# Samples' old states loaded four batches at a time, new states from spread rows on four row groups, behind the output projection

## The chip, the cores and the metric

The kernel runs on one core of a Trainium2 chip. The metric is the device time of one execution in microseconds (us), taken as the median of several runs. A core has five engines that each run their own list of instructions in order and wait for one another by semaphores: TensorE (PE in the profile, its weight loads PEld), VectorE (DVE), ScalarE (ACT), GpSimd (POOL) and SyncE (SP). In this kernel SP issues nearly all DMA transfers; a transfer that has to wait holds up all that stand behind it on SP.

## What is computed

One inference step of a decoder with two layers, width 1024. 256 new tokens of one prompt and 8 new tokens of each of 8 samples share all weights, so the kernel works on 320 tokens: columns 0 to 255 are the prompt, 256 to 319 the samples, 8 for each. Each layer projects its input, runs three mixers side by side (an SSD recurrence, a causal pooling, a sparse attention over a paged cache), projects their outputs back, and runs a convolutional FFN. The change lies in the SSD mixer, in what it does with the samples. Cut to that, for one sample `b`, with `x` of 8 heads by 64, `B` and `C` of 2 groups by 128, four heads to a group:

```
xc = x * dt                                       # 8 tokens
ac = dt * a
a_cum = cumsum(ac)
y_off = C . h0[b] * exp(a_cum)                    # old state, (8 heads, 64, 128)
y_diag = ((C . B^T) * exp(segsum(ac))) . xc
h_new[b] = h0[b] * exp(a_cum[-1]) + sum over the 8 tokens of B[t] * exp(a_cum[-1] - a_cum[t]) * xc[t]
y = (y_off + y_diag + d_skip * x) * silu(z), then rmsnorm
```

`h0[b]` comes in as `state_ssm`, `h_new[b]` goes out as `ssm_sample`. All is float32.

## The kernel before

A layer runs through these stages: norm and input projections; the mixers, interleaved by a list of steps (`ORDER`); `out_proj`, the output projection (eight tiles of 128 output rows, each 24 products `mt`: four inputs of pooling and attention first, the four of SSD behind); `ffn`. Weights come in tiles `raw` (four buffers) and are split on ACT and DVE into a high and a low part, `wh` and `wl`, or `wa` for the pair in one tile. While layer 0's `ffn` starts, `feed` also runs the cache compression of layer 1: PE products `cs` of `cache` tiles with the tiles `w` (loads on L461 and L830), which fill PE while the FFN's input is normalised.

The code goes through a scheduler: an engine's order comes from priorities that follow the program text, and `later(n)` puts what is written in its block behind work that is written up to n further on. `manual_schedule` keeps the order as written on the engine named. What stands in front on SP is thus settled when the kernel is built.

`ssd` goes through three chunks: two of the prompt, and one with the 64 sample tokens. In the third, the samples are taken in two halves `q` of four batches `j`. For each batch the old state `h` (128 rows of N by 512 columns, 256 KB) is loaded, and two products `yoh` (one for each group `g`) multiply it with the spread C rows `csp` into 32 rows of PSUM. After four batches ACT copies `yo`, PE transposes it (`yot`), and DVE scales it (`yof`) and adds it to the outputs. `ssd_norm` follows.

The new state takes `state_pre`: `bm`, the rows of B with a mask (columns `C_BM` of the constants) that leaves only one batch's 8 of 32 rows, and `hd`, the decay of the old state in place; and `state_add`: two products `sn` over 32 rows (32 of them the half's tokens, 24 of these zeros), an add `h<-h,sn` on DVE (for the keys `ha...` set to P a copy `sne` on ACT and an add on POOL), and the store `o_sss`. The helper lines in the rows: L283 matmul, L287 transpose, L290 tensor_tensor, L195 and L196 copies, L202 scaling.

The two layers differ. Layer 0 loads one batch at a time into `d2`, a pool of four buffers that other tiles share, and does everything for a batch in its turn in the third chunk. Layer 1 loads four batches with one transfer of 1 MB into `w8` (six buffers, shared with `cache`, `w`, `Ps`, `wa` and others), prepares `bm` and `hd` right there for both halves, does the first `j` of new states (`NE = 1`) in front of `ssd_norm`, and the other three behind `out_proj`, inside the start of the FFN.

A PSUM tile for these steps comes from `sst`, which takes pools in turn: `big` and `sd` in layer 0, `ns` and `sd` in layer 1.

Of the kernel before, what the change touches and what calls it, by code (L numbers as in the profile page):

```python
# [8 lines left out]
for _n, _w in (("ID", 128), ("ONE", 128), ("P", 1), ("TRI", 128), ("TRIU", 128), ("TRIS", 64), ("TRIUS", 64), ("GM", 128), ("SEL", 256),   # L9
               ("CAU", 128), ("CMP", 32), ("HS", 12), ("NEW", 8), ("WOLD", 8), ("COS", 24), ("SIN", 24), ("RW", 2),  # L10
               ("IC", 32), ("FOLD", 15), ("J1", 14), ("BM", 4), ("B8", 8)):
# [14 lines left out]
def constants():  # L26
# [38 lines left out]
    c[:96, C_BM:C_BM + 4] = (p[:96] % 32)[:, None] // 8 == np.arange(4)[None]  # L65
# [107 lines left out]
def build(ctx, tc, nc, A):  # L173
# [471 lines left out]
    def ssd(c):  # L645
# [15 lines left out]
        for i, (t0, n, tri, triu) in enumerate(CH):  # L661
# [67 lines left out]
            else:  # L729
# [5 lines left out]
                for q in range(2):  # L735
                    ph = sst(c, "yoh")
                    if l:
                        hq = w8_p.tile([128, 4, 512], F32, name="h0", tag="w8")
                        SP.dma_start(hq, A["s_ssm"][l][:, 4 * q:4 * q + 4])
                    for j in range(4):  # L740
                        if l:
                            h = hq[:, j]
                        else:
                            h = d2("h0")
                            SP.dma_start(h, A["s_ssm"][l][:, 4 * q + j])
                        c.h0[4 * q + j] = h
                        for g in range(2):
                            mm(ph[32 * j:32 * j + 32, 256 * g:256 * g + 256],
                               csp[:, g, 8 * (4 * q + j):8 * (4 * q + j) + 32], h[:, 256 * g:256 * g + 256])
                        if l == 0:  # L750
                            state_add(c, state_pre(c, bn, El, j, (q,)), xde, j, (q,))
# [12 lines left out]
                if l:  # L764
                    c.xde = xde
                    with later(SPR):
                        c.bm = [state_pre(c, bn, El, j, (0, 1)) for j in range(4)]

    def state_pre(c, bn, El, j, qs):

        bm = d1("bm")
        r = slice(32 * qs[0], 32 * qs[-1] + 32)
        sc(f"bm{c.l}{j}{qs[0]}", "D", bm[r], bn[r], cst[r, C_BM + j:C_BM + j + 1])
        for q in qs:
            h = c.h0[4 * q + j]
            tt(en(f"hd{c.l}{j}{q}", "P"), hp(h), hp(h), El[:, 1 + 4 * q + j, :, None].to_broadcast([128, 8, 64]), OP.mult)
        return bm

    def state_add(c, bm, xde, j, qs):

        pn = {q: sst(c, "sn") for q in qs}
        for g in range(2):
            for q in qs:
                r = slice(32 * q, 32 * q + 32)
# [12 lines left out]
    def states(c, js):  # L797
        for j in js:
            state_add(c, c.bm[j], c.xde, j, (0, 1))
# [531 lines left out]
```

## Time and profile before

| | |
|---|---|
| median of three runs | 1232.06 us (1231.94 to 1237.4) |
| profiled execution | 1224.47 us, of which 1222.3 us are the span |
| granted TensorE clock, mean | 0.97 |
| PE busy | 1171.7 us, 96% |
| DVE busy | 802.5 us, 66% |
| ACT busy | 536.7 us, 44% |
| POOL busy | 302.5 us, 25% |
| moved by DMA | 180.18 MB |

The profile is of one execution. PEclk is the TensorE clock that was granted, as a share of full speed (2.4 GHz; the lower level is 1.2 GHz). A float32 product shows as two records in the timeline, so "x4" of `yoh` or `sn` is two products. In a row of the timeline the matmuls are pipelined: the time of a group is from its first start to its last end.

### The profile page before, as it was taken

What the parts mean: (1) busy time and instruction counts of PE and PEld (TensorE: products, weight loads), DVE (VectorE), ACT (ScalarE), POOL (GpSimd) and SP (SyncE); (2) the same over time, 40 slices, a digit from 0 to 9 for tenths busy, and PEclk for the clock granted to TensorE, in tenths of its full rate; (3) what the DMA queues carried; (4) which work ended last, traced back from release to release, by engine and by line L of the source; (5) the groups of instructions that cost most, each with busy time, mean ns of one, the idle gap of its engine ahead of it and who ended that gap; (6) DMA issues with size and microseconds to landing.
All of it is one profiled execution on the core that took longest, in us unless ns stands there. A gap on an engine that the chain in (4) does not pass through costs nothing.

```text
span 1222.3 us, 23199 instructions
## 1 busy us (share of the span) xinstructions
PE 1171.7 (96%) x8450; PEld 1093.2 (89%) x8450; DVE 802.5 (66%) x1661; ACT 536.7 (44%) x950; POOL 302.5 (25%) x616
## 2 busy tenths in 40 slices
PE   7999998899999999999999999889999999999995
PEld 6799765599999999999999877778899999999995
DVE  4583667368756666656663688986685666666665
ACT  5445523236454444433433565433455444444431
POOL 4732222100513113311300033440342311111111
PEclk9999999699999999999999999898899999999998
DMA  7634227355555455545433445206345544445421
GB/s 277 191 100 137 76 85 252 100 161 185 175 177 199 167 168 181 159 146 184 156 104 105 154 131 189 99 27 199 119 138 171 165 143 159 152 145 158 150 72 43
DMA packets 85186, 180.18 MB, mean 147 GB/s; under 512 B 10449, under 2 KB 45009, under 8 KB 84049
## 3 DMA queue, kind: packets, MB, share of 16 engines
q1 hardware_dynamic: 84048, 176.61, 45.0%
q0 software_dynamic: 1024, 2.10, 0.6%
q8 instruction: 66, 1.08, 0.4%
q14 instruction: 48, 0.39, 0.1%
HBM read 168.97 MB, written 13.83 MB: 150 GB/s over the span
## 4 chain that ended last, share of the span: by engine, by line
PE 88%; DVE 5%; POOL 2%; ACT 2%; issue 1%; DMA 1%; SPq 1%; DVEq 0%; POOLq 0%; ACTq 0%
PE mt L283 67%; PE cs L283 5%; PE nat L283 4%; PE sn L283 1%; PE O L283 1%; PE sb L283 1%; PE sc L283 1%; PE yoh L283 1%; PE ss L283 1%; PE pe L283 1%; PE rb L283 1%; PE pT L287 1%; DMA h<-s_ssm 1%; PE sA L283 1%; DVE xt L437 1%
## 5 line engine op out<-in xcount | busy, mean ns | idle before, releaser
L342 ACT ACTIVATE wh<-raw 128x1024 fp32r<-128x1024 f32 (+2 forms) x156 | 159.9, 1026 | 199.7 <-PE mt L283 147.2
L283 PE MATMUL mt<-xh,wa 128*128 128x320 f32 x1024 | 237.2, 310 | 0.0
L283 PE MATMUL mt<-xl,wh 128*128 128x320 f32 x736 | 232.0, 315 | 0.0
L283 PE MATMUL mt<-xh,wl 128*128 128x320 f32 x736 | 231.2, 314 | 0.0
L283 PE MATMUL mt<-xh,wh 128*128 128x320 f32 x736 | 230.9, 315 | 0.2 <-ACT xh L421 0.2
L290 DVE TENSOR_TENSOR wl<-raw,wh 128x1024 fp32r<-128x1024 f32 (+2 forms) x151 | 179.5, 1189 | 68.2 <-ACT wh L342 65.5
L283 PEld LDWEIGHTS mt<-xh,wa 128*128 128x128 f32 x1024 | 174.8, 188 | 0.3
L283 PE MATMUL mt<-xl,wa 128*128 128x320 f32 x512 | 158.5, 310 | 0.0
L283 PEld LDWEIGHTS mt<-xh,wh 128*128 128x128 f32 x736 | 138.9, 189 | 5.8 <-issue 5.0
L283 PEld LDWEIGHTS mt<-xh,wl 128*128 128x128 f32 x736 | 138.8, 189 | 4.6 <-issue 3.9
L283 PEld LDWEIGHTS mt<-xl,wh 128*128 128x128 f32 x736 | 139.0, 189 | 3.2 <-issue 2.4
L290 DVE TENSOR_TENSOR wa<-raw,wa 128x1024 fp32r<-128x1024 f32 x92 | 113.5, 1234 | 37.2 <-ACT wa L342 36.9
L290 POOL TENSOR_TENSOR fa<-fa,fc 128x256 f32<-128x256 f32 (+1 forms) x128 | 82.0, 662 | 191.5 <-ACT fc L1171 136.8
L342 ACT ACTIVATE wa<-raw 128x1024 fp32r<-128x1024 f32 x92 | 96.8, 1053 | 48.4 <-DMA raw<-wg 34.9
L283 PE MATMUL mt<-act,wa 128*128 128x320 f32 x768 | 117.8, 309 | 0.0
L283 PEld LDWEIGHTS mt<-act,wa 128*128 128x128 f32 x768 | 114.0, 188 | 0.0
L283 PE MATMUL mt<-act,wh 128*128 128x320 f32 x512 | 113.2, 309 | 0.0
L283 PEld LDWEIGHTS mt<-xl,wa 128*128 128x128 f32 x512 | 96.3, 188 | 0.0
L1164 POOL COPY off<-fext 128x2 f32<-128x2 f32 x64 | 19.5, 304 | 283.2 <-DVE fext L290 283.2
L283 PEld LDWEIGHTS mt<-act,wh 128*128 128x128 f32 x512 | 85.6, 188 | 0.0
L290 DVE TENSOR_TENSOR fo<-fo,mt 128x320 f32<-128x320 f32 x112 | 54.0, 484 | 44.6 <-PE mt L283 44.3
L283 PE MATMUL mt<-act,wl 128*128 128x320 f32 x256 | 79.1, 309 | 0.0
(375 smaller groups left out, 1976.2 us busy)
## 6 DMA issues: line engine op xcount, KB each, us to landing
raw<-wg SPq DMA_DIRECT2D x168, 512.0 KB
raw<-wd SPq DMA_DIRECT2D x64, 512.0 KB
cache<-cslc SPq DMA_DIRECT2D x128, 64.0 KB
cache<-ccmp SPq DMA_DIRECT2D x96, 64.0 KB
w<-w SPq DMA_DIRECT2D x4, 1024.0 KB
o_sss<-h SPq DMA_DIRECT2D x16, 256.0 KB
o_winold<-wnat SPq DMA_DIRECT2D x16, 252.0 KB
raw<-wnb SPq DMA_DIRECT2D x8, 384.0 KB
```

The lines of the kernel that those rows point to most:

```text
L283: return PE.matmul(out, l, r, start=start, stop=stop, skip_group_check=True)
L287: return PE.transpose(out, in_, ident[:k, :k])
L290: return eng.tensor_tensor(out, a, b, op)
L342: ACT.activation(h, src, AF.Copy)
L437: DVE.scalar_tensor_tensor(t, mixo[k], w(k), rb if k else pb, op0=OP.mult, op1=OP.mult)
L1164: POOL.tensor_copy(off[:, m % 8, 0:2], ext[:, 256:258])
```

## The change

Both layers now load four old states at a time into `w8`, and the `yoh` products run in the order group outside, batch inside. The new states are computed in another form, in both layers. `state_pre` runs once for each half: a product `sp` with a selection matrix (`C_SEL`, K=64) spreads the 8 rows of each of the four batches to rows 0, 32, 64 and 96 on; that is done for `xde` (512 columns) and for `bn` (256 columns), and ACT copies both into `xs` and `bs`. The decays `hd` are as before. `bm` and its mask are gone. `states(c, q)` then makes four PSUM tiles and eight products `sn`, each of 8 rows, on four row groups in turn, in the order of the text; the adds and the stores are as before. Both halves are written behind `out_proj` under `later(100)`, in both layers; none is left in front of `ssd_norm`.

```diff
@@ -734,21 +733,14 @@
                 c.h0 = {}
                 for q in range(2):
                     ph = sst(c, "yoh")
-                    if l:
-                        hq = w8_p.tile([128, 4, 512], F32, name="h0", tag="w8")
-                        SP.dma_start(hq, A["s_ssm"][l][:, 4 * q:4 * q + 4])
-                    for j in range(4):
-                        if l:
-                            h = hq[:, j]
-                        else:
-                            h = d2("h0")
-                            SP.dma_start(h, A["s_ssm"][l][:, 4 * q + j])
-                        c.h0[4 * q + j] = h
-                        for g in range(2):
-                            mm(ph[32 * j:32 * j + 32, 256 * g:256 * g + 256],
-                               csp[:, g, 8 * (4 * q + j):8 * (4 * q + j) + 32], h[:, 256 * g:256 * g + 256])
-                        if l == 0:
-                            state_add(c, state_pre(c, bn, El, j, (q,)), xde, j, (q,))
+                    hq = w8_p.tile([128, 4, 512], F32, name="h0", tag="w8")
+                    SP.dma_start(hq, A["s_ssm"][l][:, 4 * q:4 * q + 4])
+                    c.h0[q] = hq
+                    for g in range(2):
+                        with tc.manual_schedule(engines={PE.engine}):
+                            for j in range(4):
+                                mm(ph[32 * j:32 * j + 32, 256 * g:256 * g + 256],
+                                   csp[:, g, 8 * (4 * q + j):8 * (4 * q + j) + 32], hq[:, j, 256 * g:256 * g + 256])
                     yo = d2("yo")
                     cp(f"yo{l}{q}", "A", yo, ph)
                     py = sst(c, "yot")
@@ -761,42 +753,42 @@
                     for k in range(2):
                         tt(en(f"xy{l}{q}{k}", "D"), c.xsp[k][:, :, sl], c.xsp[k][:, :, sl],
                            yof[:, 2 * k:2 * k + 2].rearrange("p m j i -> p m (j i)"), OP.add)
-                if l:
-                    c.xde = xde
-                    with later(SPR):
-                        c.bm = [state_pre(c, bn, El, j, (0, 1)) for j in range(4)]
-
-    def state_pre(c, bn, El, j, qs):
-
-        bm = d1("bm")
-        r = slice(32 * qs[0], 32 * qs[-1] + 32)
-        sc(f"bm{c.l}{j}{qs[0]}", "D", bm[r], bn[r], cst[r, C_BM + j:C_BM + j + 1])
-        for q in qs:
-            h = c.h0[4 * q + j]
+                with later(SPR):
+                    c.spread = {}
+                    for q in range(2):
+                        state_pre(c, q, bn, xde, El)
+
+    def state_pre(c, q, bn, xde, El):
+
+        sel = cst[:64, C_SEL + 128 * q:C_SEL + 128 * q + 128]
+        xs, bs = d2("xs"), d1("bs")
+        for k, (t, src, w) in enumerate(((xs, xde, 512), (bs, bn, 256))):
+            ps = sst(c, "sp")
+            mm(ps[:, :w], sel, src[:64, :w])
+            cp(f"sp{c.l}{q}{k}", "A", t, ps[:, :w])
+        c.spread[q] = xs, bs
+        for j in range(4):
+            h = c.h0[q][:, j]
             tt(en(f"hd{c.l}{j}{q}", "P"), hp(h), hp(h), El[:, 1 + 4 * q + j, :, None].to_broadcast([128, 8, 64]), OP.mult)
-        return bm
-
-    def state_add(c, bm, xde, j, qs):
-
-        pn = {q: sst(c, "sn") for q in qs}
-        for g in range(2):
-            for q in qs:
-                r = slice(32 * q, 32 * q + 32)
-                mm(pn[q][:, 256 * g:256 * g + 256], bm[r, 128 * g:128 * g + 128], xde[r, 256 * g:256 * g + 256])
-        for q in qs:
-            b = 4 * q + j
-            h = c.h0[b]
+
+    def states(c, q):
+
+        xs, bs = c.spread[q]
+        pn = [sst(c, "sn") for _ in range(4)]
+        with tc.manual_schedule(engines={PE.engine}):
+            for g in range(2):
+                for j in range(4):
+                    r = slice(32 * j, 32 * j + 8)
+                    mm(pn[j][:, 256 * g:256 * g + 256], bs[r, 128 * g:128 * g + 128], xs[r, 256 * g:256 * g + 256])
+        for j in range(4):
+            h = c.h0[q][:, j]
             if ENG.get(f"ha{c.l}{j}{q}", "D") == "P":
                 e = d2("sne")
-                ACT.activation(e, pn[q], AF.Copy)
+                ACT.activation(e, pn[j], AF.Copy)
                 tt(POOL, h, h, e, OP.add)
             else:
-                tt(DVE, h, h, pn[q], OP.add)
-            SP.dma_start(A["o_sss"][c.l][:, b], h)
-
-    def states(c, js):
-        for j in js:
-            state_add(c, c.bm[j], c.xde, j, (0, 1))
+                tt(DVE, h, h, pn[j], OP.add)
+            SP.dma_start(A["o_sss"][c.l][:, 4 * q + j], h)
 
     def ssd_norm(c):
 
@@ -1213,7 +1205,6 @@
 
     UD = (0, 3, 6)
     LAG, SE = 1, POOL
-    NE = 1
     KO = (4, 5, 6, 7, 0, 1, 2, 3)
     ROT = (0, 1, 2, 0, 1, 2, 1, 2)
     def run(c, order):
@@ -1296,14 +1287,12 @@
         pool_out(c)
         for m in range(2):
             split_into(c.mh[:, 6 + m], c.ml[:, 6 + m], c.nT[:, m])
-        if l:
-            states(c, range(NE))
         rs = ssd_norm(c)
         upd = out_proj(c, rs)
         x = load_x(xd if l else A["xT"])
-        if l:
-            with later(100):
-                states(c, range(NE, 4))
+        with later(100):
+            states(c, 0)
+            states(c, 1)
         upd, c = feed(c, l, x, upd)
     for k in range(8):
         upd(x, k)
```

Left out: `C_BM` goes from the list of constants and from the table that fills them. Line numbers behind the loops shift by 1 to 9 from before to after.

Where the instructions then stand, at three places. On SP, from layer 0's third SSD chunk to the loads for the FFN's cache work; `h_...` are the tiles of old states, `o_sss` their stores, `w_...` the tiles of the compression, `S` the prompt's state. Before:

```order
L745 DMA h_3234<-s_ssm 128x512
L830 DMA w_3739<-w 128x2048
L1027 DMA wv<-wst 128x1024
L795 DMA o_sss<-h_3198 128x512
L795 DMA o_sss<-h_3210 128x512
L795 DMA o_sss<-h_3222 128x512
L830 DMA w_3741<-w 128x2048
L795 DMA o_sss<-h_3234 128x512
L745 DMA h_3258<-s_ssm 128x512
L745 DMA h_3270<-s_ssm 128x512
```

and after:

```order
L1190 DMA o_winold<-wnat 16x4032
L1019 DMA wv<-wst 128x1024
L727 DMA o_ssp<-S_3128 128x512
L737 DMA h_3198<-s_ssm 128x2048
L737 DMA h_3226<-s_ssm 128x2048
L346 DMA raw<-wg 128x1024
L822 DMA w_3745<-w 128x2048
L822 DMA w_3747<-w 128x2048
```

The two loads of old states stand together behind `wv`, ahead of both `w` tiles, and no store stands between them.

On PE, from the last sample output `oT` of layer 0's attention to the first `mt` of `out_proj`. Before (`pl` is the pooling's product, `ss` the norm's sums):

```order
L287 MATMUL oT<-cst,os__2983 128x128
L283 MATMUL sn<-xde,bm 128x256 x4
L283 MATMUL yoh<-h_3258,csp 32x256 x2
L283 MATMUL sn<-xde,bm 128x256 x2
L283 MATMUL yoh<-h_3270,csp 32x256 x2
L283 MATMUL sn<-xde,bm 128x256 x2
L283 MATMUL yoh<-h_3284,csp 32x256 x2
L283 MATMUL yoh<-h_3296,csp 32x256 x2
L283 MATMUL ss<-cst,sq 128x1 x4
L287 MATMUL yot<-cst,yo 128x128 x4
L283 MATMUL pl<-pld,w_445 128x320 x2
```

and after:

```order
L286 MATMUL oT<-cst,os__2983 128x128
L282 MATMUL yoh<-h_3198,csp 32x256 x8
L286 MATMUL yot<-cst,yo 128x128 x4
L282 MATMUL yoh<-h_3226,csp 32x256 x8
L282 MATMUL sp<-bn,cst 128x256
L282 MATMUL sp<-xde,cst 128x512
L286 MATMUL yot<-cst,yo 128x128 x4
L282 MATMUL sp<-xde,cst 128x512
L282 MATMUL sp<-bn,cst 128x256
L282 MATMUL pl<-pld,w_445 128x320
L282 MATMUL mt<-mh,wh 128x320 x2
```

All eight batches' `yoh` now stand behind the attention's last output, the `sn` are gone from here, four `sp` have come, and the first `mt` stands ahead of the `ss`.

On PE in the start of layer 0's FFN, up to the first `mt` (`cs`, `cks`, `cvs` are layer 1's compression, `sb` the FFN's norm). Before:

```order
L283 MATMUL cs<-cache,w_3741 128x128 x16
L283 MATMUL cks<-hT,w_3734 64x160
L283 MATMUL sb<-sq,cst 128x320
L283 MATMUL cvs<-w_3734,hT 80x64 x2
L283 MATMUL cs<-cache,w_3739 128x128 x16
L283 MATMUL cs<-cache,w_3741 128x128 x16
L283 MATMUL cks<-hT,w_3734 64x160
L283 MATMUL sb<-sq,cst 128x320
L283 MATMUL cvs<-w_3734,hT 80x64 x2
L283 MATMUL sb<-sq,cst 128x320 x5
L283 MATMUL mt<-xh,wh 128x320
```

and after, from the second pair of `cs` groups on:

```order
L282 MATMUL cs<-cache,w_3747 128x128 x7
L282 MATMUL sn<-xs,bs 128x256
L282 MATMUL cs<-cache,w_3747 128x128
L282 MATMUL sn<-xs,bs 128x256
L282 MATMUL cs<-cache,w_3747 128x128
L282 MATMUL sn<-xs,bs 128x256
L282 MATMUL cs<-cache,w_3747 128x128 x7
L282 MATMUL cks<-hT,w_3740 64x160
L282 MATMUL sn<-xs,bs 128x256
L282 MATMUL cvs<-w_3740,hT 80x64 x2
L282 MATMUL sn<-xs,bs 128x256 x6
L282 MATMUL sb<-sq,cst 128x320
```

Three more `sn` stand ahead of these (behind the first `cks`), one behind the last `sb` shown, and two singly among the `mt` of `out_proj`; that makes the 16.

On SP at the same place, with what an instruction waits for (DMAHW a DMA queue, the others engines). Before, the load of the FFN's second weight tile:

```order
L1153 DMA w_4280<-wg 128x2x1024 [waits DMAHW0_49]
L1198 DMA o_winold<-wnat 16x4032 [waits DMAHW1_49]
L1201 DMA sff<-s_ffn 128x128 [waits DMAHW2_49]
L347 DMA raw<-wg 128x1024 [waits DMAHW3_49,DVE_49]
L347 DMA raw<-wg 128x1024 [waits DMAHW4_49,DVE_49]
```

and after:

```order
L346 DMA raw<-wg 128x1024 [waits DMAHW7_49,DVE_49]
L1145 DMA w_4286<-wg 128x2x1024 [waits DMAHW0_49,PE_49]
L791 DMA o_sss<-h_3198 128x512 [waits DMAHW1_49,DVE_49]
L346 DMA raw<-wg 128x1024 [waits DMAHW4_49,DMAHW2_49,Activation_49]
L346 DMA raw<-wg 128x1024 [waits DMAHW5_49,DMAHW3_49,Activation_49]
```

That load now stands behind four `raw` loads, waits for PE, and has the stores of the new states behind it.

## Rows read from the trace of the kernel before

**Rows 1.** Page: busy time of the engines (extract), and the chain's shares.
```profile
PE 1171.7 (96%) x8450; PEld 1093.2 (89%) x8450; DVE 802.5 (66%) x1661; ACT 536.7 (44%) x950; POOL 302.5 (25%) x616
...
PE 88%; DVE 5%; POOL 2%; ACT 2%; issue 1%; DMA 1%; SPq 1%; DVEq 0%; POOLq 0%; ACTq 0%
```

**Rows 2.** Windows: length, busy PE PEld DVE ACT POOL (instructions), PEclk, DMA share, GB/s.
```profile
190.00:207.50 17.50, 16.42 (x252) 10.60 (x240) 12.63 (x28) 5.41 (x14) 5.72 (x5) 1.00 0.69 233
207.50:235.20 27.70, 20.11 (x61) 11.33 (x61) 11.63 (x27) 5.40 (x14) 5.21 (x10) 0.57 0.40 130
235.20:265.10 29.90, 29.90 (x203) 29.32 (x203) 19.46 (x39) 10.12 (x15) 2.51 (x2) 1.00 0.31 91
265.10:290.50 25.40, 24.91 (x242) 22.39 (x241) 17.30 (x39) 15.38 (x31) 1.09 (x3) 1.00 0.69 241
749.50:758.00 8.50, 8.50 (x75) 6.09 (x68) 7.78 (x27) 4.16 (x11) 1.70 (x5) 1.00 0.94 341
802.20:814.50 12.30, 9.79 (x80) 6.38 (x77) 12.30 (x23) 5.96 (x16) 10.94 (x10) 1.00 0.01 2
845.60:866.10 20.50, 18.23 (x63) 14.06 (x61) 13.20 (x27) 7.32 (x12) 6.13 (x5) 0.58 0.55 189
```

**Rows 3.** Chain of waits, layer 0's stage: start, us, what.
```profile
208.19 4.00 DMA h<-s_ssm
...
224.14 2.81 DMA h<-s_ssm
```

**Rows 4.** Timeline of PE, layer 0: start, us, instruction, count, idle before.
```profile
197.51 0.69 PE L283 MATMUL sn<-xde,bm 32*128 32x256 f32 x2
198.14 0.33 PE L287 MATMUL oT<-cst,os__2899 128*128 128x128 f32 x1
...
212.24 1.92 PE L283 MATMUL yoh<-h,csp 128*32 128x256 f32 x4 [1.54 <-DMA h<-s_ssm]
...
227.00 1.92 PE L283 MATMUL yoh<-h,csp 128*32 128x256 f32 x4 [5.16 <-DMA h<-s_ssm]
228.85 1.87 PE L283 MATMUL ss<-cst,sq 128*128 128x1 f32 x8
...
233.60 1.63 PE L283 MATMUL ss<-cst,sq 128*128 128x1 f32 x12
235.16 0.56 PE L283 MATMUL mt<-mh,wh 128*128 128x320 f32 x2
```

**Rows 5.** Timeline of SP's issues: the old values' load in layer 0.
```profile
195.22 0.33 SPq L1027 DMA_DIRECT2D wv<-wst  x1
```

**Rows 6.** SP's own waits, 175 to 232 us: total, times, longest.
```profile
SPq L795 <- DVE h L290: 13.0, 6, 3.7
...
SPq L1027 <- PE pTs L287: 2.9, 1, 2.9
```

**Rows 7.** Timeline of PE, layer 1.
```profile
805.17 1.08 PE L283 MATMUL yoh<-h,csp 128*32 128x256 f32 x12
...
810.49 1.13 PE L283 MATMUL sn<-xde,bm 32*128 32x256 f32 x6 [0.22 <-DVE yof L290]
...
846.09 2.42 PE L283 MATMUL sn<-xde,bm 32*128 32x256 f32 x10
...
854.52 5.48 PE L283 MATMUL sn<-xde,bm 32*128 32x256 f32 x12
```

**Rows 8.** Tile `sn`, whole run: duration of one in ns, min/median/max.
```profile
L290 DVE TENSOR_TENSOR h<-h,sn x12: 678/686/689, 196.5 to 858.4; 128x512 f32<-128x512 f32 x12
L791 ACT ACTIVATE sne<-sn x4: 577/597/597, 210.2 to 860.0; 128x512 f32<-128x512 f32 x4
```

**Rows 9.** Timeline of SP, PE and DVE, single lines.
```profile
270.44 0.40 SPq L1153 DMA_DIRECT2D w<-wg  x1
...
279.38 7.36 PE L283 MATMUL cs<-cache,w 128*128 128x128 f32 x64
...
810.36 0.92 DVE L202 TENSOR_SCALAR bm<-bn,cst 64x256 f32<-64x256 f32 x1
```

More of the change, by code (lines that the diff above doesn't have):

```diff
@@ L10 @@
                ("CAU", 128), ("CMP", 32), ("HS", 12), ("NEW", 8), ("WOLD", 8), ("COS", 24), ("SIN", 24), ("RW", 2),
-               ("IC", 32), ("FOLD", 15), ("J1", 14), ("BM", 4), ("B8", 8)):
+               ("IC", 32), ("FOLD", 15), ("J1", 14), ("B8", 8)):
     globals()["C_" + _n] = _o
@@ L64, in constants @@
     c[:, C_J1:C_J1 + 14] = np.arange(1, 15)
-    c[:96, C_BM:C_BM + 4] = (p[:96] % 32)[:, None] // 8 == np.arange(4)[None]
     c[:64, C_B8:C_B8 + 8] = q[:, None] // 8 == np.arange(8)[None]
```

## Prediction

> **What bounds the kernel now.** I read the page first: PE is busy for 96% of the span and fills 88% of the chain of work that ended last [rows 1]. So time is won only where PE stands still or runs at its lower clock, and any product that the change adds beside a busy PE is paid in full. The table of windows shows where PE is not full. In layer 0, from 207.5 to 235.2 us, it works 20.1 of 27.7 us at a granted clock of 0.57, between a stretch and a projection that ran at 1.00; the start of layer 0's FFN (265.1 to 290.5) is full, 24.9 of 25.4 us at 1.00; the start of layer 1's FFN is the other weak place, 20.5 us at 0.58 [rows 2]. 0.57 of full speed means mostly the lower of the two levels, 1.2 instead of 2.4 GHz.
>
> Next the chain of waits and PE's timeline say what starves the first stretch: old states. PE idles for them before 212.24 and for 5.16 us before 227.00, and the chain there runs through two transfers `h<-s_ssm` [rows 3, 4]. SP's timeline and waits give the reason: `d2` has four buffers, so the fifth load of an old state stands behind the stores `o_sss` of the first four, and SP sits in these stores until DVE has added (13.0 us in six waits). The second half's first loads go out at 208.19 and the last at 224.14 [rows 3, 6]. The last `yoh` product thus runs at 227.00 and the projection's first `mt` at 235.16, 8.2 us later [rows 4].
>
> **Part 1, layer 0's loads: a gain.** With one tile of four states in `w8`, no load stands behind a store. On SP two loads of 1 MB now stand right behind `o_winold`, `wv` and `o_ssp`. `wv` is what holds them: it waits for PE to leave the old values (2.9 us once before, and out at 195.22) [rows 5, 6]. The SSD work of the prompt now stands behind some sample scores, so I let PE, and `wv`, be 2 to 3 us later: issue at 198. Ahead of the second landing lie 2 MB of states and 1 MB of others. The fastest long stretch of the trace moves 341 GB/s, the one before this stage 233 [rows 2]: 3.0 MB take 9 to 13 us. I take 10.5, nearer to the faster row because little else is queued: second landing at 208.5 (207 to 211, to 214 with a late `wv`), against 227.00.
>
> From there to the first `mt`: before, 8.2 us, of which the `ss` products (1.87 us and as much again) now stand behind the first `mt`; some 4.7 us remain, at the lower clock [rows 4]. Added are six more `yoh` products, twelve records of 0.09 us at full clock (1.08 us for 12 in layer 1), so 1.1 us, and the four spread products: 1.13 us for 6 records of 256 columns with K=32 gives 0.19 to 0.28 us a record, the two with 512 columns about twice that, together 2.3 to 3.2 us [rows 7]. At full clock this is 2.4 + 1.1 + 3 = 6.5 us, at the lower all of it doubles, 13 us. PE will have waited for the states just ahead, and in the trace it came out of such a wait at the lower level (`yoh` 1.92 us for 4 records, twice the 0.09 of layer 1 and more), to be fast again by 235.5; so I take 10, with the evacuation `yo` (0.6 us, as the copies of 128x512 [rows 8]) hidden behind the first two spread products. First `mt` at 218.5 in place of 235.2: **-16.7** (-10 to -21). PE's other work ahead of it stood until 207.5 [rows 2]; the first half's 8 `sn` at 0.62 us and 16 `yoh` records at 0.09 have left it, 6 us, and the moved SSD work gives 2 to 3 back: it is through by 204, so the landing, not PE, is next in line.
>
> **Part 2, layer 0's new states move into the projection and the FFN's start: a loss.** All 16 `sn` products now lie on a full PE: two alone among the projection's `mt`, and 14 in the FFN's start, five alone between full products, the others in runs of three and six. One alone cost 0.62 us from its start to the next (0.69 us, two records [rows 4]). In runs, the rows give 0.24 us a record on one row group (2.42 for 10) and 0.19 on two groups in turn (1.13 for 6), so 0.4 to 0.5 us a product [rows 7]. Projection: 2 x 0.62 = **+1.2**. FFN's start: 5 x 0.62 + 9 x 0.42 = **+7**. Below: 4, if the four groups overlap better than two. Above: 13, if the products fall to 0.46 us a record, as in the 5.48 us for 12 at the lower clock [rows 7]. The adds (7 of 0.69 us on DVE, the eighth by ACT and POOL [rows 8]) go onto a DVE that was busy for 17.3 of these 25.4 us [rows 2]; I let PE hide them. The decays of the eight states keep their engines, and have the projection's 30 us to run in.
>
> A single product of 32 rows between others measured 0.62 us from start to start [rows 4]. The Trainium skill, page TensorEngine Tiling (Array Packing), Key Properties, says that a change of tiling mode drains the engine, which speaks against strewing these among full products. By that rule each of the seven singles would pay again where the full products resume; at the row's 0.6 us once more, this part would be 4 us dearer and the time 1225. No row of before has a single between full products, so the trace doesn't settle it.
>
> **Part 3, a wait that the change adds.** States stay in two of `w8`'s six buffers until they are stored, and layer 1's two `w` and two `cache` tiles take the other four. So the 1 MB load of the FFN's second tile, which waited for no buffer, now waits for PE to finish a `cache` tile, and on SP all stores `o_sss` and later `raw` loads stand behind it. Before, it went out at 270.44 [rows 9]. Now it can go after the first 32 `cs` products, of which the last ended ahead of the 64 records at 279.38, some 14 us into the start [rows 9]. 1 MB at 233 GB/s is 4.5 us [rows 2], a split on two engines some 2.5: it is there about 21 us in. The `mt` of the first tile need it not: four raw tiles are issued ahead of it, and 48 products, at the projection's rate of 0.147 us (203 in 29.9 us [rows 2]), run from 32 to 39 us in. I cost it at **0**, with some 15 us of cover; were the cover gone, up to 7, the load and the split.
>
> **Part 4, layer 1.** It loaded four at a time already. Gone before the projection are the `bm` scalings (0.92 us for the longest on DVE) and two adds of 0.69 us, on a DVE that is busy for all of 12.3 us there; four `sn` go, four spread products and four ACT copies come [rows 2, 8, 9]. That is some 1 us won. At its FFN's start 16 `sn` replace 12 and lose the single-group rate; the `sn` there took 2.42 and 5.48 us [rows 7]; I put it at 1.5 us won. **-2.5** (-5 to +1).
>
> **Sum.** -16.7 + 1.2 + 7 + 0 - 2.5 = -11.0. The profiled execution took 1224.47 us, 1222.3 of it span, so it would be 1213.5; the three runs have a median of 1232.06, 7.6 above the profiled one. The change is put on the median: **1221**. Its own range, with part 1 at -12 to -20 and part 2 at 5 to 11 in all: 1215 to 1227.
>
> **Rivals.**
> A. *The groups truly overlap, and the stage keeps its clock* (1210). Four products on four row groups and four banks finish in little more than one: 0.12 us a product in the runs (a quarter of 0.48), singles as before, so the FFN's start costs +4 and the projection +1; landing at 207 and 6.5 us to the first `mt` win 21.7 us; layer 1 wins 5. Sum -21.7 + 5 - 5 = -21.7. For it: two groups in turn beat one, 0.19 against 0.24 us a record [rows 7]. Against: that is 1.3 times where two would make 2, and singles profit by nothing. In the Trainium skill, page TensorE: Matmul & The Clock Gate, Part 3, four products on four row groups measured 3.07 times the speed; by that the runs would cost some 2 us less than in my sum, which alone would give 1219. The trace has two groups at most, and they stay behind it. Chance 0.18.
> B. *The states don't come earlier* (1230). The two loads queue in order behind `wv`, and `wv` behind PE; if the moved SSD work holds PE up, or the two land one behind the other among 233 GB/s of other traffic, the second lands at 218, and the gain of part 1 shrinks to 7, which parts 2 and 4 eat. For it: `wv` did wait for PE [rows 6]. Against: it was out at 195.22, and the wait was for a step before the SSD work [rows 5]. Chance 0.13.
> C. *Slower: layer 0's FFN start loses its clock, as layer 1's did* (1240). There, `sn` products with 8 used rows beside short waits stood at the place where the granted clock fell to 0.58 [rows 2], and their records doubled from 0.24 to 0.46 us [rows 7]. If layer 0's start falls from the first `sn` run on, some 19 us of PE work take twice as long: -11 + 19 = +8. From 11 us lost on, it is slower than before. Against: PE there waits for hardly anything (24.9 of 25.4 us [rows 2]), and the `sn` lie among full `cs` products. Chance 0.07.
>
> **How the numbers follow.** Forecast 0.62, A 0.18, B 0.13, C 0.07. 0.5% is 6.2 us, about what a measurement here can tell from no change: faster means under 1225.9, slower over 1238.2. Of the forecast's 0.62, 0.54 lie below 1225.9. Faster: 0.54 + 0.18 = 0.72. Same: 0.08 + 0.12 of B = 0.20. Slower: 0.07 + 0.01 = 0.08. For 8 in 10 the range takes the forecast, most of A and half of B: 1208 to 1230.
>
> **What the changed profile would show.** Right: both `h<-s_ssm` issued by 200 and landed by 210; no idle of PE for them after that; the first `mt` of layer 0's projection between 215 and 222; the FFN's start 30 to 35 us long at a clock near 1.00; `sn` in runs at 0.3 to 0.5 us a product. Wrong: SP standing at `wv` past 203 (B); PEclk under 0.8 in layer 0's FFN start (C); PE waiting for `wa` or `raw` early in the FFN (part 3); DVE full at the FFN's start, with PE idle for `x` (part 2); runs of `sn` at 0.2 us (A).

## The result: 1.3% slower

| | before | after |
|---|---|---|
| median of 20 runs each, us | 1231.78 (1222.45 to 1239.24) | 1248.75 (1235.15 to 1261.43) |
| ratio | | 1.0127 (95%: 1.0100 to 1.0155) |
| profiled execution, us | 1224.47 | 1239.20, of which 1237.2 are the span |
| granted clock, mean | 0.970 | 0.961 |

The ratio is that of the fast runs: four of after's, 1255.0 to 1261.4 us, are left out as slow, and e2's profiled execution below was slow too. 1221 was forecast; the change costs some 16 us instead of winning 11. The page of after, in the lines of [rows 1]:

```profile
PE 1182.7 (96%) x8466; PEld 1097.5 (89%) x8466; DVE 800.2 (65%) x1654; ACT 537.5 (43%) x954; POOL 295.2 (24%) x615
...
PE 84%; DVE 5%; ACT 3%; issue 2%; POOL 2%; SPq 2%; DMA 2%; DVEq 0%; POOLq 0%; ACTq 0%
```

PE has 16 records more and is busy for 11 us longer. The lower mean clock alone makes up for about as much: 3.9% of 1237.2 us less 3.0% of 1222.3 are 11.6 us, an estimate. So the question is not only which work was added, but also what made the clock fall. The windows of after, beside [rows 2] (columns as there):

```profile
211.80:223.40 11.60, 9.77 (x51) 4.48 (x51) 7.33 (x17) 3.62 (x10) 6.88 (x7) 0.71 0.63 261
223.40:257.60 34.20, 34.20 (x228) 32.37 (x229) 20.31 (x40) 13.02 (x22) 2.50 (x2) 1.00 0.27 80
257.60:270.50 12.90, 12.41 (x152) 11.65 (x150) 6.75 (x23) 4.78 (x10) 0.10 (x1) 1.00 0.71 226
270.50:282.00 11.50, 9.05 (x55) 8.35 (x54) 5.48 (x8) 5.11 (x12) 0.99 (x2) 0.70 0.85 310
282.00:291.40 9.40, 9.40 (x55) 5.90 (x53) 5.41 (x7) 3.57 (x8) 0.83 (x1) 0.95 0.32 115
291.40:306.00 14.60, 14.60 (x69) 12.49 (x69) 9.67 (x19) 6.13 (x10) 1.53 (x3) 0.80 0.50 160
```

The projection starts at 223.4 instead of 235.2 and ends at 257.6 instead of 265.1. But the start of layer 0's FFN, 25.4 us before, lasts from 257.6 to 295.4, and in its last two thirds PE waits or runs at a clock between 0.70 and 0.95.

So that all runs can be set side by side, the table cuts the span at events that each kernel has. Columns 1 to 4 are layer 0: 1 from ACT's first `PT<-pT` to the prompt's state `S<-S,st` on DVE; 2 on to the projection's first `mixo<-mt,rb` (it holds the samples' old states); 3 on to the eighth, the projection; 4 on to the ninth `fc<-fext`, the FFN's start and its first tiles. 5 to 8 are layer 1: 5 from its `S<-S,st` to its first `mixo`; 6 its projection; 7 on to the ninth `fc`; 8 on to the last. All in us, one profiled execution each.

| | 1 | 2 | 3 | 4 | 5 | 6 | 7 | 8 | ratio to before |
|---|---|---|---|---|---|---|---|---|---|
| before | 58.1 | 54.6 | 24.5 | 101.9 | 23.7 | 24.5 | 98.1 | 230.8 | |
| after | 66.2 | 39.7 | 25.2 | 115.3 | 25.4 | 23.3 | 101.9 | 232.4 | 1.0127 |
| e5, after again | 66.3 | 48.6 | 25.2 | 111.3 | 25.4 | 23.4 | 101.9 | 232.4 | 1.012 |
| e1, columns kept | 58.1 | 37.4 | 24.5 | 111.6 | 27.9 | 23.3 | 101.9 | 232.4 | 0.998 |
| e11, e1 again | 58.0 | 34.4 | 24.5 | 112.8 | 25.4 | 23.3 | 101.9 | 232.4 | 0.997 |
| e2, loads only | 58.1 | 49.7 | 24.5 | 102.1 | 23.7 | 24.6 | 97.4 | 231.1 | 0.993 |
| e3, two w2 | 65.7 | 48.1 | 27.5 | 108.4 | 27.8 | 23.3 | 101.9 | 232.4 | 1.018 |
| e4, no update in layer 0 | 66.2 | 44.3 | 24.6 | 100.9 | 26.6 | 23.3 | 101.9 | 232.4 | 1.002 |
| e6, small adds | 66.2 | 48.7 | 25.2 | 107.2 | 25.4 | 23.3 | 101.9 | 232.4 | 1.010 |
| e7, adds on DVE | 66.2 | 48.7 | 25.2 | 114.6 | 25.5 | 23.3 | 99.8 | 232.4 | 1.014 |
| e8, in the projection | 57.9 | 34.5 | 29.8 | 102.2 | 25.4 | 28.4 | 91.8 | 231.7 | 0.985 |
| e10, e8 again | 58.1 | 34.3 | 29.8 | 102.7 | 26.9 | 28.3 | 90.2 | 232.0 | 0.987 |
| e9, e8 without columns | 66.4 | 48.6 | 29.8 | 104.1 | 25.4 | 28.3 | 91.1 | 232.4 | 1.004 |

Left out are the stretches that no edit touched: the end of layer 0's FFN (1 us longer in all) and layer 1's attention; the way from layer 0's last `fc` to layer 1's `S<-S,st` takes 199 to 216 us in one execution or another, with the clock, without a pattern among the kernels. e1 to e4 ran on a second chip, where the traced kernels lost some 30 us more in their first 128 us; the ratios are to before on the same chip.

Two things are plain from the first rows. After loses 8 us in column 1, ahead of anything that the prediction costed by more than 3; what it wins in column 2 is 15 us in one execution and 6 in the other. And columns 4 and 7, the starts of both FFNs, grew by 9 to 13 and by 4 us.

### The profile page after: what moved, and what is told of

It is laid out like the page before. It is cut to its first block, busy times and chain, and to the rows that moved or that the text cites. A ratio compares the mean times of both kernels' runs of the same rounds, so it can differ in the third digit from the quotient of the medians.

```text
span 1237.2 us, 23222 instructions
## 1 busy us (share of the span) xinstructions
PE 1182.7 (96%) x8466; PEld 1097.5 (89%) x8466; DVE 800.2 (65%) x1654; ACT 537.5 (43%) x954; POOL 295.2 (24%) x615
## 4 chain that ended last, share of the span: by engine, by line
PE 84%; DVE 5%; ACT 3%; issue 2%; POOL 2%; SPq 2%; DMA 2%; DVEq 0%; POOLq 0%; ACTq 0%
PE mt L282 64%; PE cs L282 4%; PE nat L282 4%; PE sb L282 1%; PE O L282 1%; PE sc L282 1%; SPq L460 1%; PE dec L282 1%; PE ss L282 1%; PE sn L282 1%; PE rb L282 1%; DMA h<-s_ssm 1%; PE pT L286 1%; DVE xt L436 1%; DVE G L289 1%
## 5 line engine op out<-in xcount | busy, mean ns | idle before, releaser
L289 DVE TENSOR_TENSOR wa<-raw,wa 128x1024 fp32r<-128x1024 f32 x92 | 112.8, 1226 | 28.2 <-ACT wa L341 28.0
L289 POOL TENSOR_TENSOR fa<-fa,fc 128x256 f32<-128x256 f32 (+1 forms) x128 | 77.4, 626 | 197.8 <-ACT fc L1163 143.4
```

The source lines that it names most:

```text
L289: return eng.tensor_tensor(out, a, b, op)
```

## Where the old states came too late

SP's timeline of after, layer 0 (beside [rows 5]), and its own waits from 200 to 306 us (beside [rows 6]; total, times, longest):

```profile
203.32 0.35 SPq L1019 DMA_DIRECT2D wv<-wst  x1
...
204.19 0.96 SPq L737 DMA_DIRECT2D h<-s_ssm  x2
...
224.93 0.33 SPq L815 DMA_DIRECT2D w<-w  x1
...
266.82 1.80 SPq L346 DMA_DIRECT2D raw<-wg  x4
```

```profile
SPq L791 <- DVE h L289: 16.1, 5, 7.1
SPq L815 <- PE pl L282: 14.3, 1, 14.3
SPq L1019 <- PE Os L282: 7.4, 1, 7.4
...
SPq L1145 <- PE cks L282: 2.4, 1, 2.4
```

`wv` went out 8 us later than before, and the two loads of states right behind it. PE's timeline in e5, the changed kernel again, shows what that did (start, us, instruction, idle before; beside [rows 4]):

```profile
205.30 1.07 PE L282 MATMUL Os<-cache,PT 128*32 128x64 f32 x32 [0.84 <-DVE PT L195]
...
212.01 1.81 PE L282 MATMUL yoh<-h,csp 128*32 128x256 f32 x16 [0.66 <-DMA h<-s_ssm]
214.57 1.11 PE L286 MATMUL yot<-cst,yo 128*128 128x128 f32 x4 [0.75 <-ACT yo L194]
215.61 1.94 PE L282 MATMUL yoh<-h,csp 128*32 128x256 f32 x16
...
226.28 0.90 PE L282 MATMUL mt<-mh,wh 128*128 128x320 f32 x2 [0.62 <-ACT mh L637]
226.98 0.47 PE L282 MATMUL mt<-ml,wh 128*128 128x320 f32 x1
227.25 0.47 PE L282 MATMUL mt<-mh,wl 128*128 128x320 f32 x1
```

PE reached the states with a string of short waits, and the products behind them, the projection's first too, take 0.27 us from start to start instead of 0.15. The window of e5 from its last `oT` to the first `mixo`, and that of e11:

```profile
210.70:241.50 30.80, 28.46 (x113) 19.06 (x114) 10.73 (x33) 7.53 (x19) 7.40 (x10) 0.56 0.36 138
```

```profile
203.50:220.90 17.40, 17.33 (x95) 12.37 (x94) 11.31 (x33) 6.58 (x18) 6.10 (x12) 0.90 0.48 178
```

Of the difference, 13.4 us, the lower clock takes about 12 (44% of 30.8 less 10% of 17.4, an estimate); PE's idle time is 2.3 us longer. In the first profile of after the clock rose again at 218.9, 4.5 us ahead of the projection's first product; in e5, e6, e7 and e9, all with the late states, it stayed low to some 2 us before the end of column 2.

Why PE was late is not in the text of the SSD. The change takes the four columns of the mask out of the table of constants. With that the scheduler, when the kernel is built, stands the prompt's first chunk elsewhere: in the order of after, 14 products of a projection lie between `gs` and `sC` of the samples' scores, and the first chunk's `yd` behind the scores `sA`; with four unused columns put back, `yd` stands ahead of `sC`, as before the change. PE in after, with one window, and in e11, which has the columns:

```profile
147.74 0.48 PE L286 MATMUL pct<-cst,Pc 128*128 128x128 f32 x1 [4.73 <-POOL Pc L289]
...
170.37 0.27 PE L282 MATMUL sC<-ckT,qsT 64*32 64x80 f32 x4
...
178.21 0.84 PE L282 MATMUL yd<-G,xdt 128*64 128x128 f32 x10 [0.31 <-DVE xdt L289]
```

```profile
147.20:154.00 6.80, 6.02 (x22) 5.23 (x23) 5.54 (x13) 1.58 (x2) 3.18 (x4) 0.50 0.22 60
```

```profile
150.21 0.33 PE L286 MATMUL pct<-cst,Pc 128*128 128x128 f32 x1 [0.89 <-POOL Pc L289]
...
168.58 0.66 PE L282 MATMUL yd<-G,xdt 128*64 128x128 f32 x8
169.17 0.34 PE L282 MATMUL sC<-ckT,qsT 64*32 64x80 f32 x8
```

Most of column 1's 8 us can be read there. In after PE has run out of work ahead of the transpose `pct`, which POOL's `Pc` holds up, and stands 4.73 us; in e11 products of the input projection fill that time and 0.89 us are left. From 147.2 to 154.0 the clock is at its lower level, with PE busy for 6.0 us of it, which costs about half of that, 3 us (an estimate). All seven profiles of kernels without the columns show a wait of 4.73 or 4.74 us there, and all six with them 0.89 or 0.90. Why the scheduler's order turns on the size of the table was not looked at.

**e1 and e11** put them back:

```diff
-               ("IC", 32), ("FOLD", 15), ("J1", 14), ("B8", 8)):
+               ("IC", 32), ("FOLD", 15), ("J1", 14), ("BM", 4), ("B8", 8)):
```

> The change whole, but four unused columns stay in the table of constants, so that layer 0's SSD chunks stand in PE's order where they stood before the change. In the changed kernel SP stood 7.4 us at the load wv and both loads of old states went out at 204.2, because PE reached the old values 8 us later. Theory ORDER (that lateness comes from the moved SSD work and cost layer 0's stage 8 us of its gain): wv out at 195 to 197, the second states land by 208, the projection's first product 7 to 9 us earlier than 223.4, and the whole 6 to 9 us under the changed kernel, that is within 0.5% to 0.8% above before. Rival TRAFFIC (the landing is set by what else the DMA engines carry): wv goes out earlier, but the landing stays near 215 and the time that of the changed kernel, 1.0127 of before. The start of layer 0's FFN should cost its 12 us more than before in either case.

Ratio 0.998 (0.995 to 1.001) for e1. Then, on one chip with e9 and e10:

> The kernel of e1 once more, to set it beside e10 on one chip: they differ only in where the new states stand. Theory STATES (in the FFN's start they hold back its input, in the projection only their products cost): 10 to 15 us over e10, ratio 0.994 to 1.000. If the place doesn't matter: within 4 us of e10.

Ratio 0.997 (0.993 to 1.001), against 1.012 for the kernel without the columns. Column 1 is back at 58, column 2 at 34.4. SP's timeline of e11:

```profile
190.66 0.33 SPq L737 DMA_DIRECT2D h<-s_ssm  x1
194.92 0.33 SPq L1019 DMA_DIRECT2D wv<-wst  x1
195.30 0.42 SPq L737 DMA_DIRECT2D h<-s_ssm  x1
```

The first load of states now even stands ahead of `wv`, and no `yoh` waits. ORDER holds, TRAFFIC falls. The size was missed: 6 to 9 us under the changed kernel were expected, and e1 came out some 18 under (0.998 against 1.0127); the first profile of after, from which the expectation was made, lies 9.6 us below its kernel's median. e9 does the reverse: it takes the columns out of the kernel of e8, which has the new states in the projection (below):

```diff
-               ("IC", 32), ("FOLD", 15), ("J1", 14), ("BM", 4), ("B8", 8)):
+               ("IC", 32), ("FOLD", 15), ("J1", 14), ("B8", 8)):
```

> The kernel of e8 (new states inside the output projection) without the four unused columns of the constants, so that the first SSD chunks stand behind the first sample scores again, as in the changed kernel. Theory ORDER: the prompt's state S1 comes 8 us later, PE waits for the old states once more, and the projection starts at the lower clock: from the samples' first attention work to the projection's first output 13 to 23 us more than e8's 92.4, the rest as in e8; ratio 0.996 to 1.004. Rival (the order matters little, and e8 gained by where the new states stand): ratio within 0.005 of e8's 0.985.

Ratio 1.004 (1.000 to 1.008) against 0.987 for e10 beside it: columns 1 and 2 together 115.0 against 92.4. Four unused columns are worth some 20 us (18 by the ratios of e1 and after, 22 by the medians of e9 and e10), shown twice and in both directions.

**e2** asks what the loads alone bring, with the new states as before:

```diff
-                    if l:
-                        hq = w8_p.tile([128, 4, 512], F32, name="h0", tag="w8")
-                        SP.dma_start(hq, A["s_ssm"][l][:, 4 * q:4 * q + 4])
+                    hq = w8_p.tile([128, 4, 512], F32, name="h0", tag="w8")
+                    SP.dma_start(hq, A["s_ssm"][l][:, 4 * q:4 * q + 4])
                     for j in range(4):
-                        if l:
-                            h = hq[:, j]
-                        else:
-                            h = d2("h0")
-                            SP.dma_start(h, A["s_ssm"][l][:, 4 * q + j])
+                        h = hq[:, j]
```

> The kernel before with one edit: layer 0 too loads its old states four at a time. New states as before, with the mask, in layer 0 inside the SSD stage. Theory ORDER: part 1 of the prediction by itself is right, the stage ends 10 to 17 us earlier, and nothing is added to the FFN's start, so ratio 0.985 to 0.992 of before. Rival (what follows the stage can't start earlier, because cache tiles and weights come when they come): the stage ends earlier, but the FFN's start is longer by as much, ratio 0.997 to 1.003.

Ratio 0.993 (0.990 to 0.996), a little less than expected. The FFN's start stays as before (102.1), so nothing comes too late there. Column 2 wins only 5 us of e11's 20; but it is from an execution of 1272 us, where the median is 1249, and ran at 0.69 of the clock against 0.85 in e11. How much is lost to the `sn` that still stand among the `yoh` is thus not shown.

## What made the FFN's start long

PE's and DVE's timelines of after there (beside [rows 9]):

```profile
270.99 0.71 PE L282 MATMUL sn<-xs,bs 8*128 8x256 f32 x6
274.15 0.79 PE L282 MATMUL cvs<-w,hT 128*80 128x64 f32 x4 [2.45 <-ACT hT L856]
...
283.72 0.69 PE L282 MATMUL sn<-xs,bs 8*128 8x256 f32 x2
284.35 0.49 PE L282 MATMUL cs<-cache,w 128*128 128x128 f32 x2
284.76 0.69 PE L282 MATMUL sn<-xs,bs 8*128 8x256 f32 x2
...
288.61 1.13 PE L282 MATMUL sn<-xs,bs 8*128 8x256 f32 x12
...
295.43 0.94 PE L282 MATMUL mt<-xh,wh 128*128 128x320 f32 x1
```

```profile
278.67 0.48 DVE L289 TENSOR_TENSOR x<-x,xt 128x320 f32<-128x320 f32 x1
...
283.41 0.69 DVE L289 TENSOR_TENSOR h<-h,sn 128x512 f32<-128x512 f32 x1 [0.79 <-PE sn L282]
...
285.50 0.69 DVE L289 TENSOR_TENSOR h<-h,sn 128x512 f32<-128x512 f32 x1 [0.36 <-PE sn L282]
288.60 1.23 DVE L289 TENSOR_TENSOR wa<-w,wa 128x1024 fp32r<-128x1024 f32 x1 [2.42 <-ACT wa L341]
...
291.47 1.28 DVE L289 TENSOR_TENSOR h<-h,sn 128x512 f32<-128x512 f32 x2
...
294.26 0.48 DVE L289 TENSOR_TENSOR x<-x,xt 128x320 f32<-128x320 f32 x1
```

And ACT's:

```profile
272.79 1.06 ACT L341 ACTIVATE wh<-raw 128x1024 fp32r<-128x1024 f32 x1 [1.34 <-DMA raw<-wg]
273.75 0.35 ACT L856 ACTIVATE hT<-cs,hb 128x126 f32<-128x126 f32 x1
```

Three costs stand here. PE pays the products, 0.62 us for each alone. The adds stand in DVE's order ahead of the FFN's input: between two updates `x` lie 15.6 us, in which DVE waits for `xh` and `sn`, does six adds and three splits of weights, `wa`, and waits 2.42 us for the first of these. And PE stood 2.45 us for `hT`, since ACT had two splits of late `raw` weights ahead of it; the window around that wait ran at 0.70.

**e4** takes layer 0's products and adds away and stores the decayed old states, **e6** leaves the products and lets each add cover 2 of 512 columns, **e3** takes away SP's wait of 14.3 us for the small tile `w2` that made the weights late:

```diff
 e4
+        if c.l == 0:
+            for j in range(4):
+                SP.dma_start(A["o_sss"][c.l][:, 4 * q + j], c.h0[q][:, j])
+            return
         pn = [sst(c, "sn") for _ in range(4)]
 e6
-            if ENG.get(f"ha{c.l}{j}{q}", "D") == "P":
+            if c.l and ENG.get(f"ha{c.l}{j}{q}", "D") == "P":
...
+            elif c.l:
+                tt(DVE, h, h, pn[j], OP.add)
             else:
-                tt(DVE, h, h, pn[j], OP.add)
+                tt(DVE, h[:, 0:2], h[:, 0:2], pn[j][:, 0:2], OP.add)
 e3
-        c.w2 = s1.tile([128, 416], F32, name="w2", tag="w2")
+        c.w2 = s2.tile([128, 416], F32, name="w2", tag="w2")
```

> The changed kernel without layer 0's sixteen state products and eight adds; it stores the decayed old states instead, all else (loads, spread products, decays, stores) is kept. Theory STATES: the start of layer 0's FFN falls from 37.8 us to 26 to 28, and the ratio to 1.000 to 1.005. Theory SP: it stays at 32 us or more, ratio over 1.007, since the late weights are still late.

Ratio 1.002 (0.997 to 1.006); column 4 is 100.9, a us less than before. The weights are later still (four `raw` go out 14.5 us behind the eighth `mixo`, in after 9.0), and it costs nothing: STATES.

> The changed kernel with one edit: the small tile w2 of the compression has two buffers. In the changed kernel SP stood 14.3 us at its load, until PE had done the pooling's product, with all cache loads and the FFN's first weights behind it. Theory SP (the FFN's start was long because the weights came late, ACT waited for them, hT came late, and PE stood 2.5 us and lost its clock): caches start 10 us earlier, ACT doesn't wait for raw there, PE doesn't wait for hT, the start falls from 37.8 to 30 to 33 us, ratio about 1.007. Rival STATES (the new states' products and adds are what makes it long): the start stays at 35 us or more and the ratio at 1.01 to 1.015.

Ratio 1.018 (1.011 to 1.026), no better than after. The caches did go out ahead (SP stood 24.0 us for a `raw` behind them). The FFN's start came to 31.5 us up to the first `mt`, inside theory SP's 30 to 33, but against e5's 34.5 that is 3 us, and column 4 is 108.4 against 111.3. The projection took 27.5 instead of 25.2: PE was never idle in it, but it ran at 0.92. Theory SP is worth 3 us at most, and these came back elsewhere.

> The changed kernel unaltered, as the reference for the three beside it on the same chip. Ratio 1.010 to 1.016, as first measured; the start of layer 0's FFN 37 to 38 us, that of layer 1's FFN as in the first profile.

As expected: 1.012 (1.005 to 1.019); 34.5 us up to the first `mt`, somewhat less than 37 to 38.

> The changed kernel, but each of layer 0's eight adds of a new state covers 2 of 512 columns (all on DVE), so its output there is not the full update; the sixteen products stand where they stood. Theory DVE (the adds, 0.69 us each, stand in DVE's order ahead of the next x update and hold the FFN's input back): the start of layer 0's FFN falls by 4 us or more, to 33 us or less. Theory PE (the products themselves, and the waits they bring, are the cost): it stays within 2 us of the changed kernel's, since the same products stand at the same places and the adds wait for them as before.

Ratio 1.010 (1.006 to 1.015), which tells nothing apart; the stretch does: to the first `mt` 30.8 us against 34.5 in e5, column 4 107.2 against 111.3. Column 4 as a window in e4, e6 and e5 (columns as in [rows 2]):

```profile
293.97:394.89 100.92, 100.43 (x752) 97.67 (x752) 69.03 (x124) 53.00 (x86) 22.07 (x57) 1.00 0.62 208
```

```profile
267.50:374.69 107.19, 106.51 (x780) 100.33 (x780) 69.80 (x132) 52.98 (x86) 21.76 (x57) 1.00 0.59 201
```

```profile
266.67:377.98 111.31, 109.58 (x780) 102.65 (x780) 73.03 (x131) 53.62 (x87) 24.68 (x58) 0.97 0.56 193
```

So of the 10 us between e4 and e5 the products take 6: PE is busy 6.1 us longer at the same full clock. The 4 that come with the whole adds are 1 us more in which PE stands idle, and 3 in which it is busy longer, as much as 3% of the clock are worth (an estimate). With the same whole adds column 4 is 108.4 at 0.98 (e3), 114.6 at 0.96 (e7) and 115.3 at 0.94 (after). Both theories hold a part, then, but the adds have no price of their own here: it goes by how long the clock stays low, and that differs between two executions of one kernel.

**e7** does the same for layer 1, where three adds go by POOL. POOL's timeline of after, layer 1:

```profile
864.89 3.77 POOL L289 TENSOR_TENSOR h<-h,sne 128x512 f32<-128x512 f32 x2 [37.40 <-ACT sne L787]
868.62 0.86 POOL L289 TENSOR_TENSOR x<-x,xt 128x320 f32<-128x320 f32 x1
```

```diff
-            if ENG.get(f"ha{c.l}{j}{q}", "D") == "P":
+            if not c.l and ENG.get(f"ha{c.l}{j}{q}", "D") == "P":
```

> The changed kernel, but layer 1's three adds that went by an ACT copy and a POOL add are done by DVE. In the changed kernel POOL stood before its x updates in layer 1's FFN start, and ACT waited 12 us in all for x. Theory POOL (two adds of 1.5 to 1.8 us stand ahead of POOL's first x update): from the end of layer 1's projection to the ninth FFN tile 3 to 4 us less than the changed kernel's 101.9, that is back at before's 98.2. Theory PE (the products at the lower clock are the cost, 0.6 us each alone): 101 or more.

Column 7: 99.8, between the two theories; its clock is 0.90, against 0.88 in after and 0.91 before. So 2 us of the 4 go when POOL's adds go. But before the change, too, an add stood right ahead of POOL's first `x`, and that `x` came 16.6 us into column 7, in after 14.0:

```profile
860.77 1.50 POOL L290 TENSOR_TENSOR h<-h,sne 128x512 f32<-128x512 f32 x1 [8.10 <-ACT sne L791]
862.24 1.84 POOL L290 TENSOR_TENSOR x<-x,xt 128x320 f32<-128x320 f32 x1
```

So POOL's adds do not tell after from before, and what does is not shown. A product took 1.2 us where one stood alone, at a clock of 0.50 (857 to 881 us); before, eleven of twelve stood in two runs [rows 7]. The ratio, 1.014 (1.006 to 1.021), is after's.

## A version that beats both

If the FFN's start is the wrong place, the projection is a better one: PE pays the products there too, but does not stand still for the adds. The kernel keeps the four columns, takes two batches at a time on two row groups, and has all adds on DVE (cut):

```diff
     def out_proj(c, rs):
...
             S.add(mixo[m])
+            if m in (2, 3, 4, 5):
+                i = (2, 3, 4, 5).index(m)
+                states(c, i // 2, i % 2)
...
-        pn = [sst(c, "sn") for _ in range(4)]
+        js = (2 * p, 2 * p + 1)
+        pn = {j: bigt("sn") for j in js}
...
-        with later(100):
-            states(c, 0)
-            states(c, 1)
```

> The change, with the four unused columns of the constants kept, and with the new states in both layers inside the output projection: four products and two adds for each pair of batches behind the third to the sixth of its tiles, on two row groups and two PSUM banks, all adds on DVE. If the start of the FFN is what the change costs, and the place of the SSD chunks the rest, then layer 0's stage keeps the 16 us gained with the columns kept, both FFN starts are those of before, and the projection is longer by 1 to 1.3 us for each four products, 4 to 5 us a layer: ratio 0.985 to 0.991. If the state products cost the same wherever they stand on a full PE, the projections are 9 us longer each and the ratio is 0.998 or more.

Ratio 0.985 (0.978 to 0.991). Again, beside e9 and e11:

> The kernel of e8 once more, beside the two others on one chip: ratio 0.980 to 0.990; the start of layer 0's FFN as long as before's.

Ratio 0.987 (0.983 to 0.991); 10 us under e11 in the median (1214.31 against 1224.01). The two differ in the place, and also in the grouping and in POOL's adds, which e8 gives to DVE; so the 10 us are not the place's alone. PE in e8's projection:

```profile
232.32 1.13 PE L282 MATMUL sn<-xs,bs 8*128 8x256 f32 x8
233.38 0.41 PE L282 MATMUL mt<-mh,wh 128*128 128x320 f32 x1
```

Four products cost 1.06 us, each projection 5 us in all; in layer 0's PE was busy for all of 29.8 us at 1.00, DVE for 21.5. Both FFN starts are relieved: column 4 is 102, layer 1's column 7 drops to 90 to 92, 6 to 8 us under before, which had twelve `sn` there.

## Why the prediction was wrong, step by step

- **Part 1, the loads (-16.7).** The size was right for what the change says it does: e1 and e11 win 17 and 20 us up to the projection's first output. The step that failed is "I let PE, and `wv`, be 2 to 3 us later": it was 8 (203.32 against 195.22), mostly through PE's wait of 4.73 us ahead of `pct` and the low clock that came with it. PE, which the prediction has through by 204, gave its last `oT` at 211.1. So the loads left at 204.2 instead of 198, PE waited before `yoh`, and in e5 entered the projection at 1.2 GHz. What was left is 7 us in the first profile and a loss of 2 in e5 (columns 1 and 2 together 105.9 and 114.9, against 112.7). I had named this as rival B, with 0.13, and a landing at 218; the second `yoh` ran at 215.9. The order on PE and SP was there to read, and I read it for names and not for what stands ahead of `wv`. A loose reading beside it: `yoh` in 1.92 us for 4 records is not twice 0.09 a record but five times; a group of four took 1.03 us at full clock in the same trace (at 196.56), and that is about half.
- **Part 2, the FFN's start (+7).** Measured +9 to +13. The products alone are 6 (e6 against e4), near the 7 summed. What failed is "I let PE hide them", the adds, and with it the clock near 1.00. Without whole adds the start is 4 us shorter and keeps its clock (e6). With them they stand in DVE's order ahead of `x`, PE waits, and column 4 runs at 0.94 to 0.98; that the waits bring the clock down is argued from their order in time, not tested. A DVE that is free for 8 of 25 us says nothing about who waits behind an add.
- **Part 3, the added wait (0).** Right for the wait named: SP stood 2.4 us at the 1 MB load. The longer one, 14.3 us at `w2`, I had not seen; alone it costs nothing (e4), beside the states 3 us at most (e3).
- **Part 4, layer 1 (-2.5).** Wrong in sign: +1.7, -1.2, +3.8 and +1.6 in columns 5 to 8, so +5.9. The step that failed is the forecast of 1 us won ahead of the projection and 1.5 in the FFN's start. That the spread products are what lengthened column 5 was not tested; in column 7 POOL's adds are worth 2 us (e7), but they stood ahead of `x` before as well, so the cause of its 3.8 stays open.
- **Rivals.** C forecast a slower kernel by a lost clock in layer 0's FFN start. The clock did fall there (0.84 over the whole start in after, 0.90 in e5). In column 4 that is worth about 7 of the 13 us in after and 3 of the 9 in e5 (6% and 3% of its length, an estimate), so C's mechanism had a share, smaller than its 19; in e5 more clock was lost in front of the projection. A's overlap is there: six products in 1.13 us are 0.19 us each, 2.5 times the rate on one row group [rows 7], but only seven to nine of the sixteen stand in runs.
- On the single products: a single `sn` and the full `cs` product behind it took 1.04 us together in after (283.72 to 284.76), where 0.62 were summed for the one and a `cs` in a run takes 0.23 (64 records in 7.36 us [rows 9]). So the return costs 0.2 us here, not the 0.6 that I tried. The Trainium skill, TensorEngine Tiling (Array Packing), Key Properties, says that a change of tiling mode drains the engine. The trace agrees that the return costs something; whether it is a drain it does not show.
- Two sums are slightly off: the four spread products come to 2.3 to 3.4 us, not 3.2, and the upper end of the forecast's own range to 1228.6 (-12, +11 and -2.5 on 1232.06), not 1227. Neither changes the forecast.

Sum for e5: 8.2 - 6.0 + 0.7 + 9.4 in layer 0, 5.9 in layer 1, 1 at the end of layer 0's FFN: 19, by the columns. By ratio and median it is 15 and 13 for e5, 16 and 17 for after.

## What to carry to other kernels

When a change alters an order that a scheduler makes, first lay the whole order beside the old one, from the start, and look for moves that the text doesn't ask for; an unrelated size in a table can cost as much as the edit wins. Then look where the clock was lost: here a wait of 4.7 us, and some of under 1 us, were followed by stretches at the lower level that cost as much as the waits or more. Work that is put beside a full engine is costed on each engine it touches, by what is queued behind it there: here the adds on DVE, not only the products on PE. Work whose result nobody needs soon goes where the engines behind it have slack (e8, e10).

## What was not expected of the hardware

In e5 a few waits of 0.4 to 0.8 us in a row ahead of a stage (from 205 to 215 us) went with 27 us at 1.2 GHz (212.2 to 239.5), the last 13 of them in a projection in which PE was busy for 15.2 of 15.3 us. The same instructions without these waits ran at 0.90 to 1.00 (e11, e8). But in the first profile of after the same waits, equal to within 0.1 us, went with 7 us at the lower level (212.0 to 218.9); what decides how long it lasts is open. Four products of 8 rows on two row groups in turn took 0.26 us each (e8), on four row groups 0.19, alone 0.62 (after). The way from layer 0's last `fc` to layer 1's `S<-S,st` took 199 us with 10 us at the lower level in it (before, e4, e5), and 212 with 41 (e1); why was not tried.
